# A depthwise convolution rewritten as three half-length filters, and the PSUM buffers divided anew

## Chip, cores and metric

One core of a Trainium2 chip. The kernel is written with an engine-level library: TensorE (PE) does matrix products into PSUM, VectorE (DVE), ScalarE (ACT) and GpSimd (POOL) do the rest, and SyncE (SP) issues every DMA. Each engine runs its own list of instructions in order, and waits at semaphores for the others. The metric is the device time of one execution in microseconds (us); lower is better.

## What is computed

A decoder block over 2048 tokens of width 1024, in float32. The normalised input is projected to 7680 columns; these feed a convolution branch and a sliding-window attention branch, which are gated, projected, merged and projected again.

```python
h = rmsnorm(x, norm_g[l])
proj = jnp.einsum("bsd,de->bse", h, w_in[l])
glu_in, conv_gate, q, k, v, attn_gate, merge_logits = jnp.split(proj, SPLIT_POINTS, axis=-1)
c = conformer_conv(glu_in, conv_dw_w[l], conv_dw_b[l], conv_ln_g[l], conv_ln_b[l])
y_conv = jnp.einsum("bsc,cd->bsd", c * jax.nn.silu(conv_gate), w_conv_out[l])
q = rope(q.reshape(B, S, N_Q_HEADS, HEAD_DIM), pos)
k = rope(k.reshape(B, S, N_KV_HEADS, HEAD_DIM), pos)
a = sliding_window_attention(q, k, v, attn_sinks[l])
y_attn = jnp.einsum("bsa,ad->bsd", a * jax.nn.silu(attn_gate), w_attn_out[l])
merged = g_conv * y_conv + g_attn * y_attn
x = x + jnp.einsum("bsd,de->bse", merged, w_out[l])
return rmsnorm(x, final_norm_g)
```

The part that changes is inside `conformer_conv`: for each of 1024 channels `h = a * sigmoid(b)`, then a causal filter of 31 taps along the tokens, a bias, a layer norm over the channels and a SiLU.

## The kernel before

The tokens are done in two sweeps of 1024. Every float32 operand of a product is split into a high and a low part, so one projection of 128 columns over 512 tokens (a half) is 8 x 3 matmuls of 512 columns into one PSUM tile of the pool `mm_ps`. The program `sweep` is one long list of such projections: glu, k, v, q, then gate columns (ag, cg, ma, mc) with the glu columns of the remaining channels between them, then the two branch outputs (ya, yc) and the last product (o). The order of PE's instructions is as written; the other engines' lists are ordered by the library's scheduler at build time from its own estimate of when each is ready.

`Line` (L167) paces the side work. Each step of a projection adds its estimated PE time to a clock `t`; attention blocks come due every `ATT_EVERY` = 13.8 us and background operations (`bg`) one by one every `every` us: `ROPE_EVERY` = 3.2 in the stage with q and k, `CONV_EVERY` = 2.4 afterwards. The background operations of those stages are the convolution's.

**Convolution.** A channel group c (128 channels) has its projection b evacuated by ACT as a sigmoid into `glu` and its projection a multiplied onto it by DVE (`ev_b`, `ev_a` in `glu_items`). `glu` holds 30 tokens of the sweep before, then 1024 of this. `conv_ops` then queues 31 DVE instructions of 1024 elements: one scaling with the bias (L389) and 30 multiply-adds (L393), each onto the result `cv` of the one before. POOL adds the finished `cv` to the sum for the layer norm (L399). `glu` has three slots for eight groups, so a later group's sigmoid waits until an earlier group's last tap has read its slot.

**PSUM.** There are eight banks of 512 float32: three tiles for projections (`mm_ps`), three for transposes and attention outputs (`tp_ps`), and the remaining two for one score tile (`sc_ps`). A new projection half waits until the tile three allocations earlier has been evacuated: by ACT for the gates, k/q by two DVE products (L460 to L467).

**Attention block n** (`attention`) has three steps on PE: scores `sc`; 22 us later transposes `tpp` of the probabilities; 16 us later the product `ov`. `tpp` is read by ACT (L599) and by DVE (`pt`, L242); POOL then masks `pt` into `pc` (L605), which `ov` needs. `ov` is read by ACT (L617) and DVE (L618), twice in turn.

**Weights.** `load_w` fetches a weight tile in two parts, ACT rounds each to `whi` (L253), and in the first sweep POOL computes the rest `wlo` (L242), which is also stored; in the second sweep `wlo` is loaded again and POOL is spared. A weight is prepared while the projection before it runs.

**Start.** `build_h_first` transposes the first 512 tokens: eight `tpf` tiles, each read by ACT (L363) and then by DVE (L364), before the first projection.

Of the kernel before, what the change touches and what calls it, by code (L numbers as in the profile page):

```python
# [41 lines left out]
LN_LAT = (14.0, 24.0)  # L42
LN_EVERY = 1.6
GLU_AFTER = (0, 6, 12, 16, 19, 22, 25, 28)
ROPE_EVERY = 3.2
CONV_EVERY = 2.4
ATT_EVERY = 13.8
LAT = (22.0, 16.0)
PRIO = 60
# [4 lines left out]
def hybrid_block(ctx: ExitStack, tc: tile.TileContext, x, par_d, w_in, w_conv, sinks, w_attn, w_out,  # L54
                 fin_g, rope_t, out):
    nc = tc.nc
    pe, act, dve, pool = nc.tensor, nc.scalar, nc.vector, nc.gpsimd
# [2 lines left out]
    slots = ctx.enter_context(tc.tile_pool(name="slots", bufs=1))  # L60
    stage = ctx.enter_context(tc.tile_pool(name="stage", bufs=4))
    work = ctx.enter_context(tc.tile_pool(name="work", bufs=2))
    mm_ps = ctx.enter_context(tc.tile_pool(name="mm_ps", bufs=3, space=bass.MemoryType.PSUM))
    tp_ps = ctx.enter_context(tc.tile_pool(name="tp_ps", bufs=3, space=bass.MemoryType.PSUM))
    sc_ps = ctx.enter_context(tc.tile_pool(name="sc_ps", bufs=1, space=bass.MemoryType.PSUM))
    dram = ctx.enter_context(tc.tile_pool(name="dram", bufs=1, space=bass.MemoryType.DRAM))

# [9 lines left out]
    C = [f"c{i}" for i in range(8)]  # L77
# [60 lines left out]
    def tap(c, j):  # L138
        return par[:, c, j:j + 1]
# [3 lines left out]
    def cbias(c):  # L143
        return par[:, c, TAPS + 1:TAPS + 2]
# [227 lines left out]
    def sweep(s):  # L372
# [336 lines left out]
        def gated(dst, kind, e, half, other):
            g = load_gate(kind, e, half)  # L710
            dve.tensor_tensor(out=g, in0=g, in1=other(), op=ALU.mult)
            put_split(dst, g, dve)
# [244 lines left out]
```

## Time and profile before

| quantity | value |
|---|---|
| time, median of 3 runs | 2091.1 us (2090.81 to 2091.75) |
| time of the profiled execution | 2090.34 us |
| its span, first to last instruction | 2088.4 us |
| PE busy | 2044.0 us (98%), 9256 matmuls and transposes |
| DVE busy | 1391.3 us (67%), 1901 instructions |
| ACT busy | 1032.4 us (49%) |
| POOL busy | 483.2 us (23%) |
| the 480 taps of L393 | 675.9 us of DVE, 1408 ns each |
| granted TensorE clock, mean | 0.995 |

A busy share is the share of the span in which an engine worked on something; matmuls overlap their successors, so a busy PE may still be slowed. The granted clock is TensorE's, as a share of full speed. Shares are averages over stages: the page's slices show DVE at nine tenths or more in much of the first sweep (the first half of the span) and much less from the output products on.

### The profile page before, as it was taken

The page shows a single profiled execution, that of the slowest core. Times are in us where ns is not written, and L with a number is a line of the kernel's source. Part 1 is how long each engine was busy: PE and PEld are TensorE (multiplying, and loading weights), DVE is VectorE, ACT ScalarE, POOL GpSimd, SP SyncE. Part 2 cuts the span into 40 slices and gives each one's busy share as a digit, 9 for nine tenths or more (in the row PEclk, how much of TensorE's full clock was granted, in tenths as well). Part 3 has the DMA queues.
Part 4 walks back from the last instruction along what each step waited for, and adds up shares of the span by engine and source line. Part 5 has one row for each costly group of instructions (what it writes and reads, how often), then busy time and mean ns, then how long its engine had stood idle before and what let it go on. Part 6 is the DMA issues. An engine that isn't in the chain of part 4 may idle for free.

```text
span 2088.4 us, 27452 instructions
## 1 busy us (share of the span) xinstructions
PE 2044.0 (98%) x9256; PEld 1671.7 (80%) x9256; DVE 1391.3 (67%) x1901; ACT 1032.4 (49%) x2265; POOL 483.2 (23%) x336
## 2 busy tenths in 40 slices
PE   7999999998999999999999999999999999999998
PEld 6787888886777888888888888888888888888887
DVE  4979779998988348123559596698888934341324
ACT  6221377666667646112442214766777774621222
POOL 2445433433334222243001131121111110000200
PEclk9999999999999999999999999999999999999999
DMA  7344555554455775646344456555555578574432
GB/s 250 133 144 157 178 166 157 158 163 146 148 152 182 254 238 184 202 142 221 101 151 132 141 161 204 172 158 175 175 163 164 175 225 259 162 236 146 140 119 81
DMA packets 265820, 355.90 MB, mean 170 GB/s; under 512 B 28112, under 2 KB 126544, under 8 KB 265680
## 3 DMA queue, kind: packets, MB, share of 16 engines
q1 hardware_dynamic: 265680, 354.16, 53.3%
q8 instruction: 73, 1.20, 0.2%
q14 instruction: 67, 0.55, 0.1%
HBM read 234.51 MB, written 119.54 MB: 170 GB/s over the span
## 4 chain that ended last, share of the span: by engine, by line
PE 70%; DVE 4%; issue 2%; ACT 1%; DMA 0%; POOL 0%; SPq 0%; DVEq 0%; POOLq 0%; ACTq 0%
PE o L877 9%; PE mm_mc L281 8%; PE mm_yc L281 8%; PE mm_ya L281 8%; PE mm_ma L281 7%; PE mm_ga L281 5%; PE mm_cg L281 5%; PE mm_ag L281 4%; PE mm_gb L281 4%; DVE cv L393 2%; PE mm_q_a L281 2%; PE mm_q_b L281 2%; PE ov L614 2%; PE sc L566 2%; PE mm_v L281 1%
## 5 line engine op out<-in xcount | busy, mean ns | idle before, releaser
L393 DVE SCALAR_TENSOR_TENSOR cv<-glu,par,cv 128x1024 f32<-128x1024 f32 x480 | 675.9, 1408 | 6.7
L605 POOL TENSOR_SCALAR_AFFINE_SELECT pc<-pt 128x1024 fp32r<-128x1024 f32 x60 | 102.7, 1711 | 452.9 <-DVE pt L242 419.6
L877 PE MATMUL o<-wo,mT 128*128 128x512 f32 x768 | 181.3, 394 | 0.0
L877 PEld LDWEIGHTS o<-wo,mT 128*128 128x128 f32 x768 | 143.1, 188 | 32.1
L281 PE MATMUL mm_cg<-hT,whi_cg 128*128 128x512 f32 x512 | 163.2, 400 | 4.6 <-ACT glu L415 3.0
L281 PE MATMUL mm_ma<-hT,whi_ma 128*128 128x512 f32 x512 | 162.9, 399 | 4.0 <-ACT whi_ma L253 4.0
L281 PE MATMUL mm_ga<-hT,whi_ga 128*128 128x512 f32 x512 | 161.0, 395 | 0.2 <-ACT whi_ga L253 0.2
L281 PE MATMUL mm_ag<-hT,whi_ag 128*128 128x512 f32 x512 | 160.9, 395 | 0.0
L281 PE MATMUL mm_gb<-hT,whi_gb 128*128 128x512 f32 x512 | 160.6, 395 | 0.0
L281 PE MATMUL mm_mc<-hT,whi_mc 128*128 128x512 f32 x512 | 159.6, 393 | 0.0
L281 PE MATMUL mm_yc<-uT,whi_yc 128*128 128x512 f32 x512 | 159.4, 392 | 0.0
L281 PE MATMUL mm_ya<-aT,whi_ya 128*128 128x512 f32 x512 | 158.7, 391 | 0.0
L281 PEld LDWEIGHTS mm_cg<-hT,whi_cg 128*128 128x128 f32 x512 | 95.3, 191 | 25.2 <-ACT glu L415 3.4
L281 PEld LDWEIGHTS mm_ma<-hT,whi_ma 128*128 128x128 f32 x512 | 95.1, 190 | 23.9 <-ACT whi_ma L253 4.4
L281 PEld LDWEIGHTS mm_yc<-uT,whi_yc 128*128 128x128 f32 x512 | 96.2, 188 | 21.9
L281 PEld LDWEIGHTS mm_mc<-hT,whi_mc 128*128 128x128 f32 x512 | 96.0, 188 | 21.8
L281 PEld LDWEIGHTS mm_ya<-aT,whi_ya 128*128 128x128 f32 x512 | 96.1, 188 | 20.9
L281 PEld LDWEIGHTS mm_ga<-hT,whi_ga 128*128 128x128 f32 x512 | 94.5, 188 | 20.8 <-ACT whi_ga L253 1.0
L281 PEld LDWEIGHTS mm_gb<-hT,whi_gb 128*128 128x128 f32 x512 | 94.7, 188 | 20.0
L281 PEld LDWEIGHTS mm_ag<-hT,whi_ag 128*128 128x128 f32 x512 | 94.2, 188 | 19.7 <-ACT whi_ag L253 0.3
L584 ACT ACTIVATE ss<-ss,st 128x128 f32<-128x128 f32 x256 | 99.9, 391 | 19.2 <-DVE st L579 18.6
L815 POOL TENSOR_TENSOR lmc<-lmc,mp 128x512 f32<-128x512 f32 x32 | 41.9, 1309 | 275.5 <-DVE lmc L814 267.1
(363 smaller groups left out, 4356.4 us busy)
## 6 DMA issues: line engine op xcount, KB each, us to landing
qk<-d_q SPq DMA_DIRECT2D x256, 64.0 KB, 2.7
d_a<-ss SPq DMA_DIRECT2D x128, 128.0 KB, 1.9
aT<-d_a SPq DMA_DIRECT2D x32, 512.0 KB, 6.1
qk<-d_k SPq DMA_DIRECT2D x240, 64.0 KB, 2.1
raw_gb<-in_w_in_dram SPq DMA_DIRECT2D x34, 256.0 KB, 4.0
raw_ga<-in_w_in_dram SPq DMA_DIRECT2D x34, 256.0 KB, 3.4
raw_ag<-in_w_in_dram SPq DMA_DIRECT2D x32, 256.0 KB, 3.8
d_ag<-ag SPq DMA_DIRECT2D x32, 256.0 KB, 2.1
```

Source lines behind the costliest of these rows:

```text
L281: pe.matmul(out=ps, lhsT=a, rhs=b, start=(k == 0 and i == 0), stop=(k == KC - 1 and i == 2))
L393: dve.scalar_tensor_tensor(out=cv[c], in0=glu[c][:, j:j + T], scalar=tap(c, j), in1=cv[c], op0=ALU.mult, op1=ALU.add)
L566: pe.matmul(out=o, lhsT=q[:, h, :], rhs=r, start=(j == 0), stop=(j == 1))
L584: act.activation(out=sb[:, h, :], in_=sb[:, h, :], func=AF.Exp, scale=SCALE, bias=ngm[:, h:h + 1], accum_out=den[:, h:h + 1])
L605: pool.affine_select(out=pc, in_=f(pt), pattern=[[0, 2], [0, GQ], [1, P]], compare_op=ALU.is_ge, fill=0.0, base=0, channel_multiplier=-1)
L614: pe.matmul(out=ov, lhsT=vv, rhs=pp[:, i % 2], start=(i == 0), stop=(i == nm - 1))
L815: pool.tensor_tensor(out=g, in0=g, in1=mp[e][:, half * TH:(half + 1) * TH], op=ALU.add)
L877: pe.matmul(out=ps, lhsT=a[:, c0:c0 + P], rhs=r, start=(k == 0 and i == 0), stop=(k == KC - 1 and i == 2))
```

## The change

Tokens of `glu` are stored by parity: 527 even ones, then 527 odd ones (30 + 1024 in all, halved). With the 31 taps divided into 16 even and 15 odd ones, both parities of the output follow from three filters of half length: the even taps over the odd tokens ("a"), the odd taps over the even tokens ("b"), and the sums of neighbouring taps (`tsum`) over the sum of both parities ("s"). One output parity is a and b joined with the bias, the other s minus a minus b with the bias. The result `cv` is even tokens, then odd tokens, in a half each. The layer norm works token by token and doesn't mind the order; the product with the gate (`u_op`) reads `cv` by pairs to put the tokens back in order. A group is now 50 DVE instructions of 512 to 527 elements, and their pace is set to 1.98 and 1.49 us. One of the eight PSUM banks moves from `tp_ps` to `mm_ps`: four projection tiles, two for transposes and attention outputs.

```diff
-ROPE_EVERY = 3.2
-CONV_EVERY = 2.4
+ROPE_EVERY = 1.98
+CONV_EVERY = 1.49
...
-    mm_ps = ctx.enter_context(tc.tile_pool(name="mm_ps", bufs=3, space=bass.MemoryType.PSUM))
-    tp_ps = ctx.enter_context(tc.tile_pool(name="tp_ps", bufs=3, space=bass.MemoryType.PSUM))
+    mm_ps = ctx.enter_context(tc.tile_pool(name="mm_ps", bufs=4, space=bass.MemoryType.PSUM))
+    tp_ps = ctx.enter_context(tc.tile_pool(name="tp_ps", bufs=2, space=bass.MemoryType.PSUM))
...
+    NE = (TAPS + 1) // 2
+    tsum = const.tile([P, KC, NE], F32, name="tsum")
+    dve.tensor_copy(out=tsum, in_=par[:, :, 0:TAPS:2])
+    dve.tensor_tensor(out=tsum[:, :, 0:NE - 1], in0=tsum[:, :, 0:NE - 1], in1=par[:, :, 1:TAPS:2], op=ALU.add)
...
-            def first():
-                cv[c] = slot(C[c], [P, T], F32, f"cv{s}_{c}")
-                dve.tensor_scalar(out=cv[c], in0=glu[c][:, 0:T], scalar1=tap(c, 0), scalar2=cbias(c),
-                                  op0=ALU.mult, op1=ALU.add)
-
-            def nxt(j):
-                dve.scalar_tensor_tensor(out=cv[c], in0=glu[c][:, j:j + T], scalar=tap(c, j),
-                                         in1=cv[c], op0=ALU.mult, op1=ALU.add)
...
+            def odd_tap(j):
+                if j == 0:
+                    cv[c] = slot(C[c], [P, T], F32, f"cv{s}_{c}")
+                    at["s"], at["a"] = cv[c][:, 0:TH], cv[c][:, TH:T]
+                    at["b"] = work.tile([P, TH + 1], F32, tag="fir", name=f"fir{s}_{c}", bufs=1)
+                mac(at["a"], go[:, j:j + TH], tap(c, 2 * j), (at["a"], ALU.add) if j else None)
+
+            def even_tap(j):
+                mac(at["b"], ge[:, j:j + TH + 1], tap(c, 2 * j + 1), (at["b"], ALU.add) if j else None)
+
+            def both():
+                dve.tensor_tensor(out=ge, in0=ge, in1=go, op=ALU.add)
+
+            def sum_tap(j):
+                mac(at["s"], ge[:, j:j + TH], tsum[:, c, j:j + 1],
+                    (at["s"], ALU.add) if j else (at["a"], ALU.subtract))
...
+            ops += [lambda j=j: odd_tap(j) for j in range(NE)]
+            ops += [lambda j=j: even_tap(j) for j in range(NE - 1)]
+            ops.append(both)
+            ops += [lambda j=j: sum_tap(j) for j in range(NE)]
+            ops += [lambda i=i: join(i) for i in range(2)]
...
-                act.activation(out=glu[c][:, o:o + TH], in_=ps, func=AF.Sigmoid)
+                act.activation(out=glu_of(c, half), in_=ps.rearrange("p (m o) -> p m o", o=2),
+                               func=AF.Sigmoid)
...
-                dve.tensor_tensor(out=g, in0=ps, in1=g, op=ALU.mult)
+                g = glu_of(c, half)
+                dve.tensor_tensor(out=g, in0=ps.rearrange("p (m o) -> p m o", o=2), in1=g, op=ALU.mult)
...
+            g2 = g.rearrange("p (m o) -> p m o", o=2)
+            m0 = h * (TH // 2)
+            dve.tensor_tensor(out=g2, in0=g2, in1=by_parity(cv[e])[:, m0:m0 + TH // 2], op=ALU.mult)
```

(`mac` is a scaling for the first tap of a filter and a multiply-add onto its result for the others.) PE's list is the same but for the eight layer-norm products of each sweep, which stand four rows (six matmuls) later. The other lists are ordered anew. Three places follow.

ACT at the start, before: `hT` evacuates the transposes `tpf`, `sqf` squares the second half's tokens, `whi` rounds the first weights.

```order
L363 ACTIVATE hT_0_5_129<-tpf_5_216,par 128x512
L350 ACTIVATE sqf_0_235,ssf_234<-xf_0_149 128x1024
L363 ACTIVATE hT_0_6_130<-tpf_6_223,par 128x512
L351 ACTIVATE ssf_234<-ssf_234,eps_t 128x1
L350 ACTIVATE sqf_1_240,ssf_234<-xf_1_151 128x1024
L363 ACTIVATE hT_0_7_131<-tpf_7_227,par 128x512
L351 ACTIVATE ssf_234<-ssf_234,eps_t 128x1
L350 ACTIVATE sqf_2_245,ssf_234<-xf_2_153 128x1024
```

The same place now:

```order
L369 ACTIVATE hT_0_5_132<-tpf_5_216,par 128x512
L357 ACTIVATE ssf_237<-ssf_237,eps_t 128x1
L356 ACTIVATE sqf_1_243,ssf_237<-xf_1_154 128x1024
L369 ACTIVATE hT_0_6_133<-tpf_6_223,par 128x512
L357 ACTIVATE ssf_237<-ssf_237,eps_t 128x1
L356 ACTIVATE sqf_2_248,ssf_237<-xf_2_156 128x1024
L356 ACTIVATE sqf_3_253,ssf_237<-xf_3_158 128x1024
L357 ACTIVATE ssf_237<-ssf_237,eps_t 128x1 x2
L369 ACTIVATE hT_0_7_134<-tpf_7_230,par 128x512
```

The last `hT` of the first half moved behind two more squarings.

POOL in the first sweep, in the stage with the cg gates and the glu columns of group 7, before (`wlo_cg_70` and `wlo_cg_71` are the two parts of one weight, `pc_2_3` is the mask of KV head 2, block 3):

```order
L242 TENSOR_TENSOR wlo_cg_70_4719<-raw_cg_70_4716,whi_cg_70_4718 128x512
L605 AFFINE_SELECT pc_2_3_4747<-pt_2_3_4744 128x1024
L242 TENSOR_TENSOR wlo_cg_71_4725<-raw_cg_71_4722,whi_cg_71_4724 128x512
L242 TENSOR_TENSOR wlo_gb_70_4855<-raw_gb_70_4852,whi_gb_70_4854 128x512
L605 AFFINE_SELECT pc_2_4_4887<-pt_2_4_4884 128x1024
L242 TENSOR_TENSOR wlo_gb_71_4861<-raw_gb_71_4858,whi_gb_71_4860 128x512
L242 TENSOR_TENSOR wlo_ga_70_4993<-raw_ga_70_4990,whi_ga_70_4992 128x512
L605 AFFINE_SELECT pc_2_5_5029<-pt_2_5_5026 128x1024
L242 TENSOR_TENSOR wlo_ga_71_4999<-raw_ga_71_4996,whi_ga_71_4998 128x512
```

and now:

```order
L248 TENSOR_TENSOR wlo_cg_70_4834<-raw_cg_70_4831,whi_cg_70_4833 128x512
L248 TENSOR_TENSOR wlo_cg_71_4840<-raw_cg_71_4837,whi_cg_71_4839 128x512
L651 AFFINE_SELECT pc_2_3_4864<-pt_2_3_4861 128x1024
L248 TENSOR_TENSOR wlo_gb_70_4974<-raw_gb_70_4971,whi_gb_70_4973 128x512
L248 TENSOR_TENSOR wlo_gb_71_4980<-raw_gb_71_4977,whi_gb_71_4979 128x512
L651 AFFINE_SELECT pc_2_4_5007<-pt_2_4_5004 128x1024
L248 TENSOR_TENSOR wlo_ga_70_5114<-raw_ga_70_5111,whi_ga_70_5113 128x512
L248 TENSOR_TENSOR wlo_ga_71_5120<-raw_ga_71_5117,whi_ga_71_5119 128x512
L651 AFFINE_SELECT pc_2_5_5153<-pt_2_5_5150 128x1024
```

Three times the second part of a weight moved ahead of a mask.

DVE in the same stage, around the evacuation of `tpp` and `ov` of KV head 2, before (`cv_7` are taps of group 7):

```order
L393 SCALAR_TENSOR_TENSOR cv_7_5754<-glu_7_5041,par,cv_7_5754 128x1024 x3
L242 TENSOR_TENSOR pt_2_7_5297<-tpp_2_7_5291,pt_2_7_5297 128x512
L393 SCALAR_TENSOR_TENSOR cv_7_5754<-glu_7_5041,par,cv_7_5754 128x1024 x2
L618 TENSOR_TENSOR ss_2_6_4938<-ov_2_6_5320,ss_2_6_4938 64x256
L393 SCALAR_TENSOR_TENSOR cv_7_5754<-glu_7_5041,par,cv_7_5754 128x1024
L618 TENSOR_TENSOR ss_2_6_4938<-ov_2_6_5320,ss_2_6_4938 64x256
```

and now (`fir` is the filter b):

```order
L248 TENSOR_TENSOR pt_2_7_5428<-tpp_2_7_5422,pt_2_7_5428 128x512
L403 SCALAR_TENSOR_TENSOR cv_7_5933<-glu_7_5165,par,cv_7_5933 128x512
L403 SCALAR_TENSOR_TENSOR fir_7_5934<-glu_7_5165,par,fir_7_5934 128x513
L403 SCALAR_TENSOR_TENSOR cv_7_5933<-glu_7_5165,par,cv_7_5933 128x512
L403 SCALAR_TENSOR_TENSOR fir_7_5934<-glu_7_5165,par,fir_7_5934 128x513
L664 TENSOR_TENSOR ss_2_6_5059<-ov_2_6_5452,ss_2_6_5059 64x256
L403 SCALAR_TENSOR_TENSOR cv_7_5933<-glu_7_5165,par,cv_7_5933 128x512
L664 TENSOR_TENSOR ss_2_6_5059<-ov_2_6_5452,ss_2_6_5059 64x256
```

Two whole taps became four half ones, one whole tap one half one; the filters a and b alternate.

## Rows read from the trace of the kernel before

**Rows 1.** Page, part 1: busy time of every engine.

```profile
PE 2044.0 (98%) x9256; PEld 1671.7 (80%) x9256; DVE 1391.3 (67%) x1901; ACT 1032.4 (49%) x2265; POOL 483.2 (23%) x336
```

**Rows 2.** Tile views: ns min/median/max, first to last start; each sweep apart.

```profile
L281 PE MATMUL mm_kb<-hT,whi_kb x32: 387/392/398, 56.9 to 67.5; 128*128 128x512 f32 x32
...
L281 PE MATMUL mm_cg<-hT,whi_cg x256: 387/393/652, 392.9 to 564.8; 128*128 128x512 f32 x128
...
L281 PE MATMUL mm_ma<-hT,whi_ma x256: 387/392/796, 595.5 to 707.6; 128*128 128x512 f32 x128
...
L281 PE MATMUL mm_ya<-aT,whi_ya x256: 387/389/398, 801.6 to 889.2; 128*128 128x512 f32 x128
...
L281 PE MATMUL mm_kb<-hT,whi_kb x32: 387/392/404, 1107.0 to 1117.6; 128*128 128x512 f32 x32
...
L281 PE MATMUL mm_cg<-hT,whi_cg x256: 387/392/484, 1432.0 to 1590.1; 128*128 128x512 f32 x128
...
L281 PE MATMUL mm_ma<-hT,whi_ma x256: 387/393/482, 1617.3 to 1723.3; 128*128 128x512 f32 x128
...
L281 PE MATMUL mm_ya<-aT,whi_ya x256: 387/389/398, 1816.5 to 1903.7; 128*128 128x512 f32 x128
```

**Rows 3.** Waits of PE: total us, times, longest.

```profile
PE mm_ma L281 <- ACT whi_ma L253: 4.0, 1, 4.0
PE mm_q_b L281 <- DVE rb_q__1_1524 L467: 3.4, 1, 3.4
PE mm_cg L281 <- ACT glu L415: 3.0, 1, 3.0
PE mm_ga L281 <- POOL wlo_ga L242: 2.5, 3, 1.2
...
PE tpv L499 <- ACT vs L519: 2.1, 1, 2.1
PE mm_cg L281 <- POOL wlo_cg L242: 2.0, 1, 2.0
PE mm_cg L281 <- ACT cg L434: 1.7, 1, 1.7
```

**Rows 4.** Windows: stretch, length, busy us PE PEld DVE ACT POOL, clock, DMA.

```profile
200.00:205.00 5.00, 5.00 (x19) 4.03 (x18) 4.86 (x4) 1.66 (x3) 3.70 (x3) 0.78 0.52 158
...
630.00:635.00 5.00, 4.87 (x11) 3.38 (x12) 4.94 (x7) 1.98 (x5) 4.64 (x3) 0.50 0.14 34
```

**Rows 5.** Line views of DVE: ns min/median/max, first to last start.

```profile
L393 DVE SCALAR_TENSOR_TENSOR cv<-glu,par,cv x240: 1253/1285/2392, 54.0 to 658.8; 128x1024 f32<-128x1024 f32 x120
...
L858 DVE SCALAR_TENSOR_TENSOR y<-y,yrs,gb x17: 746/1285/1286, 1033.6 to 2084.6; 128x1024 f32<-128x1024 f32 x15, 128x512 f32<-128x512 f32 x2
...
L322 DVE TENSOR_SCALAR x<-x,rs x16: 479/482/490, 993.8 to 1072.7; 128x512 f32<-128x512 f32 x16
```

**Rows 6.** Timeline of DVE: start, duration; a tap and what follows it.

```profile
509.05 1.28 DVE L393 SCALAR_TENSOR_TENSOR cv<-glu,par,cv 128x1024 f32<-128x1024 f32 x1
510.24 0.16 DVE L579 SCALAR_TENSOR_TENSOR st<-st,nsink 128x4 f32<-128x4 f32 x1
```

**Rows 7.** Windows of 100 us, first and second sweep; columns as in Rows 4.

```profile
400.00:500.00 100.00, 97.27 (x459) 79.24 (x458) 94.71 (x122) 68.05 (x159) 37.60 (x24) 1.00 0.51 157
...
1500.00:1600.00 100.00, 100.00 (x477) 82.98 (x476) 93.34 (x132) 73.56 (x172) 15.93 (x9) 1.00 0.57 170
```

**Rows 8.** Timeline: a `tpp` tile written on PE, and read last on DVE.

```profile
486.45 0.92 PE L594 MATMUL tpp<-ident_r,ss 128*128 128x128 f32 x3
...
504.81 0.68 DVE L242 TENSOR_TENSOR pt<-tpp,pt 128x512 fp32r<-128x512 f32 x1
```

**Rows 9.** Timeline: POOL's mask and weight, and the matmul that waited.

```profile
549.48 2.07 POOL L605 TENSOR_SCALAR_AFFINE_SELECT pc<-pt 128x1024 fp32r<-128x1024 f32 x1 [7.51 <-DVE pt L242]
551.52 2.23 POOL L242 TENSOR_TENSOR wlo_cg<-raw_cg,whi_cg 128x512 fp32r<-128x512 f32 x1
...
553.80 0.80 PE L281 MATMUL mm_cg<-hT,wlo_cg 128*128 128x512 f32 x1 [1.96 <-POOL wlo_cg L242]
```

**Rows 10.** Timeline of PE at the start: the last `tpf` transposes.

```profile
18.11 0.66 PE L361 MATMUL tpf<-ident_r,xf 128*128 128x128 f32 x4 [0.50 <-DVE hT L364]
```

More of the change, by code (lines that the diff above doesn't have):

```diff
@@ L29 @@
 HALO = TAPS - 1
+NG = (HALO + T) // 2
 HD = 64
@@ L385, in conv_ops, with mac, join @@
             ops = []
-            def first():
-                cv[c] = slot(C[c], [P, T], F32, f"cv{s}_{c}")
-                dve.tensor_scalar(out=cv[c], in0=glu[c][:, 0:T], scalar1=tap(c, 0), scalar2=cbias(c),
-                                  op0=ALU.mult, op1=ALU.add)
-            def nxt(j):
-                dve.scalar_tensor_tensor(out=cv[c], in0=glu[c][:, j:j + T], scalar=tap(c, j),
-                                         in1=cv[c], op0=ALU.mult, op1=ALU.add)
-                if j == TAPS - 1:
+            ge, go = (glu[c][:, i * NG:(i + 1) * NG] for i in range(2))
+            at = {}
+            def mac(out_, src, w, init):
+                if init is None:
+                    dve.tensor_scalar(out=out_, in0=src, scalar1=w, scalar2=None, op0=ALU.mult)
+                else:
+                    dve.scalar_tensor_tensor(out=out_, in0=src, scalar=w, in1=init[0], op0=ALU.mult,
+                                             op1=init[1])
+            def odd_tap(j):
[11 more added lines that the diff above has]
+                    (at["s"], ALU.add) if j else (at["a"], ALU.subtract))
+            def join(i):
+                if i == 0:
+                    dve.scalar_tensor_tensor(out=at["a"], in0=at["a"], scalar=cbias(c), in1=at["b"][:, 1:],
+                                             op0=ALU.add, op1=ALU.add)
+                else:
+                    dve.scalar_tensor_tensor(out=at["s"], in0=at["s"], scalar=cbias(c),
+                                             in1=at["b"][:, 0:TH], op0=ALU.add, op1=ALU.subtract)
+                if i == 1:
                     if not conv_done:
@@ L402, in nxt, with by_parity, glu_of @@
                         line.start(ln_chain())
-            ops.append(first)
-            for j in range(1, TAPS):
-                ops.append(lambda j=j: nxt(j))
-            return ops
+            ops += [lambda j=j: odd_tap(j) for j in range(NE)]
[3 more added lines that the diff above has]
+            ops += [lambda i=i: join(i) for i in range(2)]
+            return ops
+        def by_parity(ap):
+            return ap.rearrange("p (o m) -> p m o", o=2)
+        def glu_of(c, half):
+            m0 = HALO // 2 + half * (TH // 2)
+            return by_parity(glu[c])[:, m0:m0 + TH // 2]
         def glu_items(c):
@@ L412, in ev_b @@
                     glu[c] = slot(glu_slot[c], [P, HALO + T], F32, f"glu{s}_{c}")
-                    pool.tensor_copy(out=glu[c][:, 0:HALO], in_=glu_halo[:, c, :])
-                o = HALO + half * TH
-                act.activation(out=glu[c][:, o:o + TH], in_=ps, func=AF.Sigmoid)
+                    pool.tensor_copy(out=by_parity(glu[c])[:, 0:HALO // 2], in_=glu_halo[:, c, :].rearrange(
+                        "p (m o) -> p m o", o=2))
+                act.activation(out=glu_of(c, half), in_=ps.rearrange("p (m o) -> p m o", o=2),
+                               func=AF.Sigmoid)
             def ev_a(half, ps):
-                g = glu[c][:, HALO + half * TH:HALO + (half + 1) * TH]
-                dve.tensor_tensor(out=g, in0=ps, in1=g, op=ALU.mult)
+                g = glu_of(c, half)
+                dve.tensor_tensor(out=g, in0=ps.rearrange("p (m o) -> p m o", o=2), in1=g, op=ALU.mult)
                 if half == 1:
                     if s + 1 < NSWEEP:
-                        pool.tensor_copy(out=glu_halo[:, c, :], in_=glu[c][:, T:T + HALO])
+                        pool.tensor_copy(out=glu_halo[:, c, :].rearrange("p (m o) -> p m o", o=2),
+                                         in_=by_parity(glu[c])[:, TH:NG])
                     line.bg.extend(conv_ops(c))
@@ L707, in sweep @@
         aT, uT = [[None] * KC, [None] * KC], []
[L709 to L712, printed above, removed]
         def a_op(e, h):
@@ L720, in u_op @@
         def u_op(e, h):
-            gated(uT[h][e], "cg", e, h, lambda: cv[e][:, h * TH:(h + 1) * TH])
+            g = load_gate("cg", e, h)
+            g2 = g.rearrange("p (m o) -> p m o", o=2)
+            m0 = h * (TH // 2)
+            dve.tensor_tensor(out=g2, in0=g2, in1=by_parity(cv[e])[:, m0:m0 + TH // 2], op=ALU.mult)
+            put_split(uT[h][e], g, dve)
             stored.add(("u", e, h))
```

## The prediction

> **What bounds the kernel now.** I began with the busy shares. PE is busy in 98% of the span and DVE in 67% [rows 1], so a change that shortens DVE's work can gain only where PE waits or runs slowly because of DVE. A mean cannot show that, so next I compared the two sweeps, which send the same list of products through PE. From the first matmul of `mm_kb` to the first of `mm_ya` the first sweep takes 801.6 - 56.9 = 744.7 us, the second 1816.5 - 1107.0 = 709.5 us [rows 2]. The first loses 35.2 us. By stage, with the second sweep subtracted: k, v, q and ag gates (kb to cg) 336.0 - 325.0 = 11.0; cg and the glu groups among it (cg to ma) 202.6 - 185.3 = 17.3; ma and mc (ma to ya) 206.1 - 199.2 = 6.9. This is what the change can win, for the second sweep has no wait of PE worth a row.
>
> The waits say what PE lost it to [rows 3]. Three kinds stand out. A projection waits for a PSUM tile that DVE or ACT has yet to evacuate (`rb_q` 3.4, `glu` 3.0, `cg` 1.7). A projection waits for a weight that ACT or POOL has yet to prepare (`whi_ma` 4.0, `wlo_ga` 2.5, `wlo_cg` 2.0). A transpose waits for v's copy on ACT (2.1). [...]
>
> Behind all three kinds stands DVE's queue. In 400 to 500 us DVE is busy 94.71 of 100 us [rows 7]. A `tpp` tile written at 486.45 had its last reader on DVE at 504.81, and was held 19 us [rows 8], longer than the 13.8 us between attention blocks. POOL's queue inherits the delay: its mask waited 7.51 us for that DVE result at 549.48, the second part of a weight stood behind the mask, and PE waited 1.96 us for it at 553.80 [rows 9]. The second sweep at 1500 to 1600 us has DVE at 93.34 and PE at 100 [rows 7]; there POOL is busy 15.93 us instead of 37.60, as the weights' low parts are loaded.
>
> **The change, part by part.** *The filter.* Before, a group costs 31 instructions of 1285 ns (median of the taps; the first, a scaling, is taken as one of them), 39.8 us [rows 5]. After, it is 48 two-input instructions of half the length and two scalings. The same instruction over 512 elements takes 746 ns on the rows of the output, a scaling 482 ns [rows 5]: 48 x 0.746 + 2 x 0.482 = 36.8 us. Filters a and b alternate in DVE's new list, so that neighbours no longer depend on each other; where a tap was followed by an independent instruction, that began 0.09 us before the tap's end [rows 6], which for 31 instructions is 2.8 us less. That leaves 34.0, a saving of 5.8 us a group (3.0 if nothing overlaps, 7.3 if all 50 do). For the seven groups or so that run between `mm_kb` and `mm_ya` that is 41 us of DVE in 710, some 6 points of its share. It lies beside PE's work; its worth is only the waits it ends.
>
> The rows show a fixed cost of 2 x 746 - 1285 = 207 ns an instruction, so halving the length costs 19 more of these, 3.9 us, and fewer elements win more. [...]
>
> *Order by parity.* ACT's sigmoid, DVE's product (16 of each a sweep) and the gate's product in `u_op` now step 2 KB between neighbours. No row shows this. It costs nothing at the least, and at most I take the slowest tap against its median, 2392 / 1285 = 1.9 times [rows 5]: 1.3 us more DVE a group, which leaves most of the saving. I take nothing, since no row shows a pattern that is dearer. [...]
>
> *Fourth projection tile.* A projection half is 24 matmuls, about 5.5 us. With four tiles a half waits for the evacuation one half earlier, 5.5 us of slack more, against waits of at most 3.4 us. [...]
>
> *Two transpose tiles.* At the start, eight `tpf` tiles go through; already with three the last waited 0.50 us [rows 10]. Each of the six after the second may wait for one more evacuation: between 0 and 6 x 0.5 = 3 us; I take 1.5, on the path, for the first projection stands behind them. ACT's new order (the last `hT` behind two more squarings) is inside that. In the blocks a tile now returns after 13.8 us. With holds of 19 us PE would wait up to 5 us in a block; with DVE less behind, holds should fall below 13.8. I take 1 us, of 0 to 10 (two such blocks).
>
> *New order on POOL.* Three times the second part of a weight now precedes the mask. That is the wait of [rows 9] and its two neighbours. What is late next is `pc`, needed only 16 us later.
>
> *Sums of taps at the start.* Two small DVE instructions before the last scaling of the tokens; under 0.3 us, inside the 1.5.
>
> **Sum, against the profiled execution.** Start +1.5. Kb to cg -7.5 of 11.0 (the q waits and their slow clock go, v's 2.1 us stays; -3 to -11). Cg to ma -13 of 17.3 (-5, PSUM waits alone, to -17). Ma to ya -4.5 of 6.9 (0 to -6). Transpose tiles +1. Second sweep 0, as PE never waits in it. Together -22.5: 2090.3 - 22.5 = 2067.8, and the median of the runs lies 0.8 above the profiled time: **2068.6, say 2068 us**.
>
> **The rivals.** *Stall-free.* The first sweep becomes the second. For it: DVE in the second sweep is as busy as now, and PE doesn't wait. Against: POOL's contention stays. It gives 2091.1 - 35.2 + 1.5 = 2057; chance 0.17.
>
> *Only the PSUM waits go.* DVE's instructions don't get shorter in sum (3.0 saved a group, or strided operands eat it), or DVE fills the time that PE no longer gives it: PE's stalls are also DVE's chance to catch up. Then weights stay late. From 11.0 go 5, from 17.3 some 6, against +2.5 for the tiles: 2091.1 - 8.5 = 2082.6; chance 0.15.
>
> *Slower: the ring of two.* The tiles of `tpp` and `ov` still are held over 13.8 us. Place: the blocks of the first sweep. [...] It decides where holds stay above 13.8 us, which needs DVE as late as now; the rows speak against that in most blocks, for holds of 19 us come only where DVE is at 95%. Chance 0.06.
>
> *It doesn't do what it says*: gain and costs cancel, weights as late as before, the start +3, transposes some more: within 4 us of 2091; chance 0.06.
>
> **How the numbers follow.** The forecast, some two thirds of the loss won, has the remaining 0.56 and its own range 2060 to 2078. For 8 in 10 the range takes in the stall-free case and the one with only the PSUM waits, 2053 (sweep one is a little lighter, since the first block of each KV head has no predecessor) to 2085. A measurement of this kernel tells about 0.2%, 4.2 us, from no change. Faster by more: forecast, stall-free and PSUM case together 0.88; same 0.06; slower 0.06.
>
> **What would show it.** In the changed profile: kb to ya of the first sweep at 715 to 725 us; no wait of PE for `rb_q`, `glu` or `cg`; `wlo` waits gone at cg and ga of group 7; the taps at 0.66 to 0.75 us each and their total near 16 x 34 = 544 us where it was 676 plus the first taps; holds of `tpp` below 14 us; the first projection 1 to 2 us later than 18.5; the second sweep unchanged to a microsecond. Wrong would make it: PE waiting for `tpp` or `ov` tiles, taps above 0.8 us, or `whi` and `wlo` waits where they are now.

## The result, and the profile after

The changed kernel takes 2098.7 us (median of 5 runs, 2098.48 to 2099.99) where the kernel before takes 2091.1 us beside it: ratio 1.0038, 95% interval 1.0027 to 1.0048. It is 7.6 us slower; forecast were 2068 us, and a range from 2053 to 2085. The profiled execution has a span of 2096.7 us, 8.3 more than before, and its mean granted clock is 0.995, as before.

The page's first part, beside [rows 1]:

```profile
PE 2046.0 (98%) x9256; PEld 1672.6 (80%) x9256; DVE 1331.6 (64%) x2207; ACT 1050.0 (50%) x2269; POOL 446.4 (21%) x336
```

DVE is busy 60 us less. So the change did lighten DVE, and yet no time was won. The first and last starts of `mm_kb` and `mm_ya`, each sweep apart (answering [rows 2]):

```profile
L287 PE MATMUL mm_kb<-hT,whi_kb x32: 387/392/398, 59.7 to 70.2; 128*128 128x512 f32 x32
L287 PE MATMUL mm_ya<-aT,whi_ya x256: 387/389/398, 808.4 to 895.9; 128*128 128x512 f32 x128
L287 PE MATMUL mm_kb<-hT,whi_kb x32: 387/392/404, 1113.8 to 1124.4; 128*128 128x512 f32 x32
L287 PE MATMUL mm_ya<-aT,whi_ya x256: 387/389/398, 1824.9 to 1912.1; 128*128 128x512 f32 x128
```

The start is 2.8 us later, the first sweep from `mm_kb` to `mm_ya` takes 748.7 us instead of 744.7, the second 711.1 instead of 709.5: 2.8 + 4.0 + 1.6 = 8.4, the whole difference.

PE's waits (us in total, times, longest), answering [rows 3]:

```profile
PE ov L660 <- DVE ss L664: 7.0, 8, 1.4
PE tpp L640 <- DVE pt L248: 7.0, 4, 2.3
PE mm_gb L287 <- POOL wlo_gb L248: 5.4, 3, 3.5
PE tpv L545 <- ACT vf L547: 4.4, 1, 4.4
...
PE mm_ga L287 <- POOL wlo_ga L248: 2.7, 1, 2.7
```

The waits for `rb_q`, `glu` and `cg` are gone. In their place stand 14 us of waits for the two buffers of `tpp` and `ov`, and the waits for weights that POOL prepares (`wlo`) are 8.9 us in sum, where they were 7.9. One of those `tpp` tiles, as in [rows 8], written on PE and read last on DVE:

```profile
497.01 0.70 PE L640 MATMUL tpp<-ident_r,ss 128*128 128x128 f32 x4
...
514.23 0.69 DVE L248 TENSOR_TENSOR pt<-tpp,pt 128x512 fp32r<-128x512 f32 x1
```

It is held 17.9 us, against 19 before. Of the 32 `tpp` tiles of the first sweep ten are held for more than 13.8 us, where it was five before. (In the second sweep of the kernel before, with DVE at 93.34 [rows 7], none was held for more than 7.8 us.) DVE serves an urgent evacuation about as late as before, although it has less to do. From 400 to 500 us [rows 7] DVE is at 89.7 instead of 94.7, and PE at 94.6 instead of 97.3. The taps, by line view (ns min/median/max) and from the page (total us, mean ns):

```profile
L403 DVE SCALAR_TENSOR_TENSOR cv<-glu,tsum,cv x256: 730/752/1833, 93.3 to 1676.6; 128x512 f32<-128x512 f32 x128
L403 DVE SCALAR_TENSOR_TENSOR cv<-glu,par,cv x240: 714/741/1849, 56.7 to 1652.7; 128x512 f32<-128x512 f32 x120
```

```profile
L403 DVE SCALAR_TENSOR_TENSOR cv<-glu,tsum,cv 128x512 f32<-128x512 f32 x256 | 210.0, 820 | 5.0
L403 DVE SCALAR_TENSOR_TENSOR cv<-glu,par,cv 128x512 f32<-128x512 f32 x240 | 197.9, 825 | 0.2
L403 DVE SCALAR_TENSOR_TENSOR fir<-glu,par,fir 128x513 f32<-128x513 f32 x224 | 187.4, 837 | 1.0
```

The medians are what was forecast (0.75 us), the means are not: a tail up to 1.85 us adds some 80 ns to each. Times 720 that is 58 us, the same 59 us as before (1408 - 1285 = 123 ns, times 480). So the taps' regular time fell and their tail did not. Where the tail comes from is seen by laying DVE beside POOL:

```profile
82.66 0.75 DVE L403 SCALAR_TENSOR_TENSOR cv<-glu,par,cv 128x512 f32<-128x512 f32 x1
83.32 1.79 DVE L403 SCALAR_TENSOR_TENSOR fir<-glu,par,fir 128x513 f32<-128x513 f32 x1
85.03 1.78 DVE L403 SCALAR_TENSOR_TENSOR cv<-glu,par,cv 128x512 f32<-128x512 f32 x1
86.73 0.74 DVE L403 SCALAR_TENSOR_TENSOR fir<-glu,par,fir 128x513 f32<-128x513 f32 x1
...
83.15 3.11 POOL L248 TENSOR_TENSOR wlo_q_a<-raw_q_a,whi_q_a 128x512 fp32r<-128x512 f32 x2 [1.79 <-issue]
```

While POOL does its two subtractions, 83.15 to 86.26, two taps take 1.8 us; those ahead and behind take 0.75. The whole traces say the same. Of the 480 taps before, 84 take over 0.1 us more than the median, by 0.72 us on the mean; of the 720 now it is 74, by 0.80 us. Every one of them overlaps an instruction of POOL. Of the taps that overlap none, the longest takes 1289 ns before and 756 ns now.

### The profile page after: what moved, and what is told of

Same layout as the page of the kernel before. It is cut to its first block, busy times and chain, and to the rows that moved or that the text cites. A ratio compares the mean times of both kernels' runs of the same rounds, so it can differ in the third digit from the quotient of the medians.

```text
span 2096.7 us, 27858 instructions
## 1 busy us (share of the span) xinstructions
PE 2046.0 (98%) x9256; PEld 1672.6 (80%) x9256; DVE 1331.6 (64%) x2207; ACT 1050.0 (50%) x2269; POOL 446.4 (21%) x336
## 4 chain that ended last, share of the span: by engine, by line
PE 75%; DVE 17%; ACT 5%; issue 1%; DMA 1%; SPq 0%; POOL 0%; DVEq 0%; ACTq 0%; POOLq 0%
PE o L922 8%; PE mm_mc L287 8%; PE mm_yc L287 8%; PE mm_ya L287 8%; DVE cv L403 6%; PE mm_gb L287 6%; PE mm_ga L287 6%; PE mm_ma L287 6%; PE mm_cg L287 4%; PE mm_ag L287 4%; PE mm_q_a L287 4%; DVE fir L403 3%; PE mm_q_b L287 3%; PE ov L660 2%; PE sc L612 2%; PE mm_v L287 2%
## 5 line engine op out<-in xcount | busy, mean ns | idle before, releaser
L403 DVE SCALAR_TENSOR_TENSOR cv<-glu,tsum,cv 128x512 f32<-128x512 f32 x256 | 210.0, 820 | 5.0
L403 DVE SCALAR_TENSOR_TENSOR cv<-glu,par,cv 128x512 f32<-128x512 f32 x240 | 197.9, 825 | 0.2
L403 DVE SCALAR_TENSOR_TENSOR fir<-glu,par,fir 128x513 f32<-128x513 f32 x224 | 187.4, 837 | 1.0
L651 POOL TENSOR_SCALAR_AFFINE_SELECT pc<-pt 128x1024 fp32r<-128x1024 f32 x60 | 79.9, 1332 | 413.6 <-DVE pt L248 413.6
L287 PEld LDWEIGHTS mm_ga<-hT,whi_ga 128*128 128x128 f32 x512 | 94.6, 188 | 19.9
L287 PEld LDWEIGHTS mm_cg<-hT,whi_cg 128*128 128x128 f32 x512 | 94.7, 190 | 19.7
```

Source lines behind the costliest of these rows:

```text
L287: pe.matmul(out=ps, lhsT=a, rhs=b, start=(k == 0 and i == 0), stop=(k == KC - 1 and i == 2))
L403: dve.scalar_tensor_tensor(out=out_, in0=src, scalar=w, in1=init[0], op0=ALU.mult, op1=init[1])
L651: pool.affine_select(out=pc, in_=f(pt), pattern=[[0, 2], [0, GQ], [1, P]], compare_op=ALU.is_ge, fill=0.0, base=0, channel_multiplier=-1)
```

## The experiments

**The two parts apart.** `e1_conv_alone` is the changed kernel with the rings of before, `e2_rings_alone` the kernel before with the changed rings. The edit is that of e1; e2 makes it the other way round.

```diff
-    mm_ps = ctx.enter_context(tc.tile_pool(name="mm_ps", bufs=4, space=bass.MemoryType.PSUM))
-    tp_ps = ctx.enter_context(tc.tile_pool(name="tp_ps", bufs=2, space=bass.MemoryType.PSUM))
+    mm_ps = ctx.enter_context(tc.tile_pool(name="mm_ps", bufs=3, space=bass.MemoryType.PSUM))
+    tp_ps = ctx.enter_context(tc.tile_pool(name="tp_ps", bufs=3, space=bass.MemoryType.PSUM))
```

> The convolution, the parity order and the paces of the change, with three projection tiles and three for transposes as before. Theory R (the ring of two ate the gain): DVE's list is 60 us shorter in all, 31 us of that between mm_kb and mm_ya of the first sweep, so without the ring of two PE's waits for tpp, ov (7.0 us each) and tpf (2.4) go, and the time falls below before: 2078 to 2086. Theory D (DVE's relief is not what ends PE's waits in the first sweep): waits of before stay and the time is 2089 to 2093, no change. Theory S (the parity access costs more than the filter gives): 2094 to 2100, as the change itself, since the rings were innocent.

> The convolution of before, with four projection tiles and two for transposes and attention outputs. Theory R: the longer taps of before (1285 ns, none can be interrupted) hold the two tiles longer than 13.8 us in many blocks, so this is the slowest: 2100 to 2110, with tpp and ov waits above 14 us in sum. Theory D: the rings give +3 to +8 on their own, 2094 to 2099, and with the change at 2098.7 the convolution then costs about nothing or little. Theory S: 2089 to 2093, the waits that the fourth projection tile ends weigh up those of the ring of two.

Measured: e1 2095.7 us, ratio 1.0020 (1.0011 to 1.0029); e2 2094.4 us, 1.0014 (1.0005 to 1.0022). The parts add up: +4.5 and +3.1, together +7.6. Theory R falls: without the ring of two the convolution is still slower than before. The rings cost what the start costs: in e2 the first `mm_kb` comes at 60.4 us, 3.5 later, and the sweep from there to `mm_ya` takes 745.5, 0.8 more. Their waits in the blocks only take the place of the projections' waits. Theory D's range has e2; e1 lies 2.7 us above it, and inside theory S's range, so that e3 has to decide on S. The convolution alone makes the sweep 2.7 us longer although DVE is lighter.

**The parity access.** `e3_no_stride` is the changed kernel with contiguous access (the copies of the 30 tokens of the sweep before and the sigmoid and product are made contiguous too).

```diff
-            return by_parity(glu[c])[:, m0:m0 + TH // 2]
+            return glu[c][:, 2 * m0:2 * m0 + TH]
...
-            dve.tensor_tensor(out=g2, in0=g2, in1=by_parity(cv[e])[:, m0:m0 + TH // 2], op=ALU.mult)
+            dve.tensor_tensor(out=g, in0=g, in1=cv[e][:, h * TH:(h + 1) * TH], op=ALU.mult)
```

> The changed kernel, but glu is written token after token and the gate's product reads it so (sigmoid, product, halo copies and u_op contiguous as before), with the three filters as they are: they then run over the two halves of the row instead of the parities, so the values of the convolution branch are others; the instructions and their sizes stay. Theory S: sigmoid back at 0.60 us, product at 0.69, 13 us of DVE and 15.6 us of ACT less in all, and the time falls by 5 to 10 us to 2089 to 2094. Theories R and D: the sigmoid and product are shorter by as much, but PE's waits hardly move: 2095 to 2099.

Measured: 2099.7 us, 1.0039 (1.0025 to 1.0053), as slow as the change. The sigmoid alone was 15.6 us shorter in sum, as these rows show (the change, then e3):

```profile
L459 ACT ACTIVATE glu<-mm_gb 128x512 f32<-128x512 f32 x32 | 34.7, 1085 | 4.2 <-PE mm_gb L287 4.0
```

```profile
L458 ACT ACTIVATE glu<-mm_gb 128x512 f32<-128x512 f32 x32 | 19.1, 597 | 6.7 <-PE mm_gb L287 6.5
```

So the stride has a price on its engines and none in the time. Theory S falls.

**What DVE's relief is worth.** `e4_26_taps` and `e5_12_taps` are the kernel before with fewer taps. The edit is that of e4; e5 has `range(1, 12)`. Both stretch the paces as well.

```diff
-            for j in range(1, TAPS):
+            for j in range(1, TAPS - 5):
```

> The kernel before with 26 of the 31 taps in every group, at paces stretched by 31/26 so that a group is due as long as before; nothing else. It leaves out five taps, so the values of the convolution are others. DVE gets 5 x 1.285 x 8 = 51 us lighter in each sweep, a little more than the 46 that the prediction gave the new filter (31 us measured between mm_kb and mm_ya). Theory R (relief of DVE is worth what was predicted, the ring took it): 2065 to 2075. Theory D (the first sweep's waits are not ended by relief): 2085 to 2091.

> The kernel before with 12 of the 31 taps in every group, at paces stretched by 31/12; it leaves out 19 taps, so the values of the convolution are others. DVE gets 19 x 1.285 x 8 = 195 us lighter in each sweep, six times the 31 us that the change took from the stage between mm_kb and mm_ya. Theory L (DVE's load makes PE wait in the first sweep, as the prediction had it, and 31 or 51 us were too few): the first sweep becomes as fast as the second, 2055 to 2062. Theory P (POOL's work on the weights in the first sweep makes the waits, directly or by slowing DVE and ACT beside it): much of the loss stays, 2070 to 2082.

Measured: e4 2081.5 us, 0.9950 (0.9937 to 0.9962), 9.8 less; e5 2056.7 us, 0.9833 (0.9817 to 0.9849), 34.7 less. e4 fits neither range and lies between them: a relief larger than the one the filter was to give brings 10 us, less than half of the 24 that the prediction had. In e4 the stages up to cg hardly move (334.5 us instead of 336.0), the gain is from cg to ma. e5 is as theory L has it: with 195 us less, the first sweep runs as fast as the second. So DVE's taps are part of the cause. But here both the amount of work and its meetings with POOL have shrunk.

**POOL's work.** In `e6_lo_loaded` the first sweep loads the weights' low parts; `e7_lo_loaded_after` is the same in the changed kernel; in `e8_lo_beside` POOL subtracts nevertheless, into a tile that nobody reads (the last line, which e8 alone has).

```diff
-                split_lo(lo, raw, hi, pool)
+                nc.sync.dma_start(out=f(lo), in_=d_z[kh])
+                split_lo(idle, raw, hi, pool)
```

> The kernel before, taps and rings untouched, but in the first sweep the low part of every weight is loaded by DMA from a block of zeros in DRAM instead of computed by POOL (it leaves out the low parts' values; their loads, stores and products stay). This is what the second sweep does. DVE's load stays at 93 to 95 of 100 us. Theory P: kb to ya falls from 744.7 to 709 to 720 and the time to 2056 to 2068. Theory L: only the wlo waits go (7.4 us in sum with the clock behind them perhaps 10): 2080 to 2086.

> The changed kernel with the low parts of the first sweep loaded from a block of zeros, as in the run before this one. Theory P: the filter's relief has nothing left to win, so that the difference between this and the run before is the start alone, +3 (the eight tpf tiles through two buffers), and perhaps the 1.6 us at mm_ma of the second sweep: 2060 to 2072. Theory L: 2090 to 2095, and tpp and ov waits stay.

> As e6 (PE takes a loaded block of zeros as the low part), but POOL still does its subtraction for every weight of the first sweep, into a tile that nobody reads. POOL is as busy as before; no product waits for it. If POOL hurts by being late (its list is in order, and weights stand behind masks): as e6, 2056 to 2068. If it hurts by running beside DVE and making DVE's instructions longer (taps of 2.0 to 2.4 us where the median is 1.285): as before, 2083 to 2090.

Measured: e6 2061.8 us, 0.9859 (0.9844 to 0.9874); e7 2065.6 us, 0.9876 (0.9861 to 0.9891); e8 2100.1 us, 1.0042 (1.0027 to 1.0057). All 31 taps are done in e6, and from `mm_kb` to `mm_ya` the first sweep takes 710.1 us: of its 35 us of loss 0.6 are left (the time fell by only 29.6, since the first `mm_kb` comes 6.3 us later there). e7 against e6: +3.8, of which 2.8 at the start and 1.7 at `mm_ma` of the second sweep; the new filter has nothing to win there. And e8 brings the loss back, without a product that waits for POOL; it lies above both of its ranges. The stretch from `mm_kb` to `mm_ya` (us, then busy us of PE, PEld, DVE, ACT, POOL, clock) before, in e6 and in e8:

```profile
56.90:801.60 744.70, 719.09 (x3265) 585.94 (x3264) 600.73 (x732) 415.21 (x919) 280.78 (x186) 0.99 0.54 169
```

```profile
63.20:773.30 710.10, 707.21 (x3265) 582.02 (x3264) 538.22 (x731) 416.36 (x919) 104.22 (x73) 1.00 0.68 218
```

```profile
61.90:813.00 751.10, 720.30 (x3265) 584.90 (x3264) 598.74 (x732) 415.87 (x919) 281.59 (x186) 0.99 0.65 207
```

The same work of DVE (731 or 732 instructions) keeps it busy 62 us less when POOL's subtractions are gone, and 60 us more when they are back. (So DVE's load did not stay at 93 to 95 of 100 us in e6, as expected there: from 400 to 500 us it is 87.29.) Some of e8's waits of PE:

```profile
PE mm_q_b L289 <- DVE rb_q__1_1589 L475: 3.4, 1, 3.4
PE mm_cg L289 <- ACT glu L423: 3.0, 1, 3.0
PE mm_cg L289 <- ACT cg L442: 2.2, 2, 1.7
PE tpv L507 <- ACT vs L527: 2.1, 1, 2.1
```

These are the waits of before [rows 3], three of them to a tenth of a microsecond, and no row of that view names POOL. Up to `mm_ma` the stages of e8 are as long as before (336.1 and 202.5 us, against 336.0 and 202.6): the `wlo` waits on POOL are gone there, and PE loses as much to other waits. So POOL's lateness with a weight is not what makes the loss there; its work beside DVE is. The rest of e8's time says nothing of POOL. Its first `mm_kb` comes 5.0 us later, behind a wait of 5.3 us for `whi_ga` on ACT, which e6 has too; and from `mm_ma` to `mm_ya` it is 6.4 us longer, with waits of 3.6 us for `wlo_ma` by DMA and 5.9 for the evacuation of `mc` on ACT.

**Taking the meeting away.** The trace of before has DVE instructions that no meeting prolonged. Line view, ns min/median/max, of the product that reads PSUM (11 of the 32 overlap an instruction of POOL):

```profile
L419 DVE TENSOR_TENSOR glu<-mm_ga,glu x32: 660/691/693, 33.7 to 1617.5; 128x512 f32<-128x512 f32 x32
```

The tap, which has both operands in SBUF, goes from 1253 over 1285 to 2392 [rows 5]. The half-length filters a and s fit a PSUM bank each, one after the other. `e9_acc_psum` gives them the bank of the fourth projection tile, `e10_acc_sbuf` is its control with that bank unused (of the diff it has the change to `mm_ps` alone).

```diff
-    mm_ps = ctx.enter_context(tc.tile_pool(name="mm_ps", bufs=4, space=bass.MemoryType.PSUM))
+    mm_ps = ctx.enter_context(tc.tile_pool(name="mm_ps", bufs=3, space=bass.MemoryType.PSUM))
+    acc_ps = ctx.enter_context(tc.tile_pool(name="acc_ps", bufs=1, space=bass.MemoryType.PSUM))
...
-                    at["s"], at["a"] = cv[c][:, 0:TH], cv[c][:, TH:T]
+                    at["a"] = at["s"] = acc_ps.tile([P, TH], F32, tag="acc", name=f"acc{s}_{c}")
...
-            ops.append(both)
+            ops += [lambda: join(0), both]
             ops += [lambda j=j: sum_tap(j) for j in range(NE)]
-            ops += [lambda i=i: join(i) for i in range(2)]
+            ops.append(lambda: join(1))
```

(`join` reads the accumulator and `fir` and writes the halves of `cv`.)

> The changed kernel with filters a and s accumulated in the PSUM bank that the fourth projection tile had (three projection tiles, two for transposes, one accumulator; a is joined to b before s starts from it). The rows show that DVE's operations with one operand in PSUM are not prolonged (the product with mm_ga at most 693 ns around a median of 691, pt from tpp 687 on the mean) where those with both in SBUF reach 1.4 to 2.4 times. Theory C (it is DVE and POOL beside each other on SBUF that make the first sweep's waits): 34 of 50 instructions of a group can't be prolonged any more, their mean falls from 0.82 to about 0.75 us, POOL's subtractions come down to 1.3 us, and the time to 2075 to 2092. Theory L (PE waits for what stands ahead in DVE's list, whatever runs beside): as the control, 2097 to 2103.

> Control for the run before: the changed kernel with three projection tiles and two for transposes, accumulators in SBUF as in the change, the eighth bank unused. Both theories: the start costs 3 and the q waits of 3.4 come back, 2097 to 2103.

Measured: e9 2055.3 us, 0.9830 (0.9817 to 0.9844), 36 us faster than before and below its expected range; e10 2099.5 us, 1.0041 (1.0028 to 1.0053). All of PE's waits in e9:

```profile
PE tpf L368 <- DVE ident_r L119: 8.4, 1, 8.4
PE tpf L368 <- DVE hT L371: 2.4, 4, 0.7
PE tpf L368 <- DVE xf L361: 1.9, 2, 1.3
```

They all lie ahead of the first projection. From `mm_kb` to `mm_ya` PE never waits, and the waits for two transpose tiles are gone too, though there are still two. The taps of e9, and the same place as above:

```profile
L404 DVE SCALAR_TENSOR_TENSOR acc<-glu,tsum,acc x256: 735/756/757, 90.1 to 1630.0; 128x512 f32<-128x512 f32 x128
L404 DVE SCALAR_TENSOR_TENSOR acc<-glu,par,acc x240: 717/744/757, 57.1 to 1604.7; 128x512 f32<-128x512 f32 x120
L404 DVE SCALAR_TENSOR_TENSOR fir<-glu,par,fir x224: 712/746/1794, 57.8 to 1611.9; 128x513 f32<-128x513 f32 x112
```

```profile
80.42 1.73 DVE L404 SCALAR_TENSOR_TENSOR fir<-glu,par,fir 128x513 f32<-128x513 f32 x1
82.08 0.74 DVE L404 SCALAR_TENSOR_TENSOR acc<-glu,par,acc 128x512 f32<-128x512 f32 x1
82.73 0.74 DVE L404 SCALAR_TENSOR_TENSOR fir<-glu,par,fir 128x513 f32<-128x513 f32 x1
83.40 0.74 DVE L404 SCALAR_TENSOR_TENSOR acc<-glu,par,acc 128x512 f32<-128x512 f32 x1
84.06 1.12 DVE L404 SCALAR_TENSOR_TENSOR fir<-glu,par,fir 128x513 f32<-128x513 f32 x1
...
80.31 1.29 POOL L249 TENSOR_TENSOR wlo_q_a<-raw_q_a,whi_q_a 128x512 fp32r<-128x512 f32 x1 [3.17 <-DMA d_k<-hl_k]
83.11 1.51 POOL L249 TENSOR_TENSOR wlo_q_a<-raw_q_a,whi_q_a 128x512 fp32r<-128x512 f32 x1 [1.51 <-DMA raw_q_b<-in_w_in_dram]
```

The same instruction over 512 or 513 elements: accumulating in PSUM it never exceeds 757 ns, though 111 of those 496 taps overlap an instruction of POOL; accumulating in SBUF (`fir`) it reaches 1794, when POOL runs. e9 also joins a to b before filter s starts, and the build ordered its lists anew; no run has these two alone.

**Amount or meeting.** In e9 DVE also became lighter, by 53 us against e10. `e12_acc_heavy` adds taps of the kind that took 757 ns at most in e9.

```diff
-            ops += [lambda j=j: sum_tap(j) for j in range(NE)]
+            ops += [lambda j=j: sum_tap(j) for j in list(range(NE)) + list(range(8, NE))]
```

> As e9, but the last eight taps of filter s are done twice in every group (58 instructions instead of 50, paces shortened by 50/58), so the values of the convolution are others. DVE gets 8 x 0.75 x 8 = 48 us heavier in each sweep and is as heavy as in the kernel before, with the instructions added being such as POOL can't prolong. Theory C (what counts is whether DVE and POOL meet on SBUF, not the amount of DVE's work): 2054 to 2062, no waits of PE worth a row. Theory L (the amount counts; e9 won since it made DVE 53 us lighter): most of what e9 won is lost again, 2075 to 2090.

Measured: 2055.1 us, 0.9831 (0.9815 to 0.9848). The stretch from `mm_kb` to `mm_ya` as above, the change first, then e4, then e12 (cut 0.2 us after its own start and end):

```profile
59.70:808.40 748.70, 719.13 (x3265) 585.92 (x3264) 569.29 (x882) 414.68 (x915) 258.86 (x186) 0.99 0.54 168
```

```profile
57.00:792.80 735.80, 716.33 (x3266) 585.43 (x3265) 544.07 (x692) 415.79 (x919) 278.82 (x186) 0.99 0.55 171
```

```profile
60.30:766.60 706.30, 706.30 (x3265) 582.65 (x3264) 574.27 (x945) 415.08 (x915) 239.48 (x186) 1.00 0.57 178
```

e12 has DVE busy 5 us longer than the change, in 42 us less time, and PE is busy in all of it. DVE's share is 81% in e12, as in the kernel before (600.7 of 744.7 us). And e4, with 30 us less of DVE than e12, still loses 26 us against the second sweep. So DVE's amount of work alone doesn't decide, and theory C holds. Where the meetings stay, the amount does count: e4 and e5 won 9.8 and 34.7 us by it.

**The start.** `e11_acc_start` was to give back the 3 us at the start.

```diff
+            ring, tag = (mm_ps, "mm") if half == 0 and k % 2 else (tp_ps, "tp")
```

> As e9, and at the start every second tpf transpose of the first half goes to a projection tile, of which none is in use yet. Both theories: the first mm_kb comes 2.5 to 3.5 us earlier than in e9 (back at 56 to 57 us), and the time is lower by as much. By theory C 2072 to 2089.

A miss: 2057.4 us, 0.9839 (0.9826 to 0.9853), 2.0 slower than e9. The wait of `tpf` for `hT` was gone, but this row came in:

```profile
PE mm_ga L288 <- ACT whi_ga L260: 5.4, 1, 5.4
```

With the transposes free, the build ordered ACT's list anew and the second projection's weight came late; `mm_kb` began at 61.2 us instead of 60.3.

## Why the prediction was wrong

**The step that failed is the first one: "Behind all three kinds stands DVE's queue."** It read DVE's busy share as the cause of the late evacuations, and so gave a lighter DVE the waits as a gain. The trace of before held the counter-example, and the prediction quoted it [rows 7]: the second sweep has DVE at 93.34 and no wait. What differs between the sweeps is POOL, 37.60 against 15.93. It makes DVE's own work longer: from `mm_kb` to `mm_ya` 732 instructions of DVE take 600.7 us in the first sweep, and 728 take 539.5 us in the second. This was set aside as something that speaks against the stall-free rival ("POOL's contention stays"), when it was what made the waits. e6, e8 and e12 show it from three sides: without POOL's subtractions 0.6 us of the loss are left with all of DVE's instructions in place, with them the loss is there even when nobody needs their result, and with two of the three accumulators out of SBUF there is none at a load above that of the change. Of the prediction's own signs of being wrong these came: waits for `tpp` and `ov`, taps above 0.8 us on the mean, and `wlo` waits.

In e9 a multiply-add took 757 ns at most with one operand in PSUM, beside POOL or not, and up to 1794 ns beside POOL with both in SBUF. Weighed against the change, this says that three filters in SBUF meet POOL as before, and the taps of the change do reach 1849 ns.

**The filter's saving** was sized nearly right. By durations a group fell from (675.9 + 16.0) / 16 = 43.2 us to 653.4 / 16 = 40.8, that is 2.4 instead of the 3.0 without overlap. DVE's busy time fell by 59.7 us while the durations in sum fell by only some 24 (39 off the filters; 13 back on the product with `mm_ga`, 2 on the gate's). The other 36 us I put down to overlap, 2.2 us a group, where 2.8 was worked out. (With 0.09 us for all 50 instructions the prediction's upper bound of 7.3 would be 7.5.) What the forecast of 0.66 to 0.75 us a tap missed is that it compared medians, and the tail is not shortened with the instruction: a prolonged tap lost 0.72 us at the old length and 0.80 us at half of it, and there are nearly as many (84 and 74).

**The worth of the saving** was the mis-sized term: -25 (7.5, 13 and 4.5 in three stages) against the measured +4.0, +1.5 and -1.5. e4 measures a relief of 51 us a sweep: -10. For the 31 us that DVE was busy less in the first sweep one would by that estimate expect some -6, and e1 shows +4.5.

Why DVE serves urgent work no sooner, one place shows, the wait of `tpv` for v's copies on ACT. Before, then the change (in the second, 12.7 us of the filters' instructions stand between 82.66 and 95.39):

```profile
79.36 12.35 DVE L393 SCALAR_TENSOR_TENSOR cv<-glu,par,cv 128x1024 f32<-128x1024 f32 x8
91.63 0.55 DVE L502 TENSOR_TENSOR vd<-tpv,vf 128x384 f32<-128x384 f32 x1
...
92.21 0.40 ACT L513 CAST vd<-vd 128x256 fp32r<-128x256 f32 x1 [10.62 <-DVE vd L502]
```

```profile
95.39 0.55 DVE L548 TENSOR_TENSOR vd<-tpv,vf 128x384 f32<-128x384 f32 x1
...
95.98 0.40 ACT L559 CAST vd<-vd 128x256 fp32r<-128x256 f32 x1 [11.46 <-DVE vd L548]
98.94 0.88 PE L545 MATMUL tpv<-ident_r,vs 128*128 128x128 f32 x3 [4.39 <-ACT vf L547]
```

Ahead of v's evacuation stood eight taps; now there are more and shorter ones, of the same length together. Two of them are the prolonged ones shown above, beside POOL (before, the eight take 2.1 us more than eight medians). So shorter taps ended DVE's work earlier, but not this urgent instruction. That the build fills the room ahead of an urgent instruction with whatever taps are ready elsewhere too, and that all of the +2.7 us of e1's first sweep comes from such places, is argued, not shown.

**Fourth projection tile.** Right as far as it went: the waits for `rb_q`, `glu` and `cg` are gone, in e2 as in the change (a wait of 1.7 and 1.1 us for `ra_q` stands at `mm_gb` instead). They were worth next to nothing: e10, which differs from the change in the fourth tile alone, takes 2099.5 us against its 2098.7. The prediction's sum also counts on a slow clock behind the `q` waits, and no run shows what that is worth by itself. The stretches of [rows 4] follow PE's waits for `rb_q` and `whi_ma`. From `mm_kb` to `mm_ya` of the first sweep the granted clock was 0.50 for 17.1 us before, in four pieces of 3.4 to 6.8 us behind waits of 2.0 to 4.0 us. In the change it was 0.50 for 17.1 us again, behind waits of 2.1 to 4.4 us for `tpv`, `wlo_gb` and `tpp`.

**Two transpose tiles.** The mechanism was right twice and the size wrong twice. The start cost 2.8 us (e2: 3.5) where 1.5 was taken and 3 was the bound. (The two sums of taps, taken as under 0.3 us from no row, took 0.22 and 0.28 us.) In the blocks 14.0 us of waits came where 1 was taken, since holds stayed above 13.8 us. That is the "ring of two" rival's point of decision, and its direction came true, but not its mechanism as the cause: e1 without that ring loses too, and e9 with it has no such wait.

**POOL's order.** The second parts moved ahead of the masks as described, but PE's waits for a `wlo` of POOL were 8.9 us in sum, where they had been 7.9. So the masks' place in POOL's list was not what made most of them.

**Parity access at no cost.** The time bears it out (e3). The rows don't: product 685 to 1094 ns, sigmoid 598 to 1085. The value taken for DVE's row was wrong, the bound of 1.3 us a group held (0.8).

**Second sweep unchanged.** It became 1.6 us longer at `mm_ma`, with waits for `wlo_ma` by DMA and for `whi_ma`. e1, e7 and e10 have it, e2, e3 and e9 have not. It goes with the new filter in SBUF and the strided sigmoid together; what exactly delays ACT there stays open.

## What to carry to other kernels

Ask of a late engine not only how busy it is but beside whom it works: compare two stretches with the same load and a different neighbour, and look at the maximum of a line beside its median. Here DVE and POOL both streamed from SBUF, and an accumulator that DVE keeps in PSUM took the two apart (757 ns at most, where the same multiply-add in SBUF reached 1794); what the half-length filter was worth is that its accumulator fits a bank. Relief of a busy engine can bring much less than its size: 51 us less of DVE's work in a sweep brought 10 us.

## What the runs showed of the hardware

A DVE multiply-add over 512 elements takes the same 0.75 us with its accumulator in PSUM (median 744 to 756 ns) as in SBUF (741 to 752). A scaling into PSUM is dearer: 754 ns, where one into SBUF takes 481 to 490. Writing or reading pairs of elements two kilobytes apart costs DVE 60% (685 to 1094 ns, one operand in PSUM) and ACT 81% (598 to 1085); with only one of two SBUF inputs so strided, 3% (median 688 to 709; the mean of 744 has one instruction of 1800 ns in it, which ran beside POOL). Removing the meetings also shortens POOL: 258.9 us busy between `mm_kb` and `mm_ya` in the change, 239.5 in e12.
